# Up projections of two feed-forward stages by seven block products in place of eight, in a decoder layer on one Trainium2 core

## The chip, the cores and the metric

The kernel runs on one core of a Trainium2 chip. The metric is the device time of one execution in microseconds. Three runs of the kernel before took 1301.07 to 1302.55 us, with a median of 1301.34 us.

## The reference

One layer of a decoder: 512 tokens of width 1024, all in float32. Four residual stages follow one another, each closed by a layer norm. The first and the last are SwiGLU feed-forward stages of inner width 2816; between them lie a token mixer (two kinds of attention) and an attention into 256 memory rows. Cut to what matters here:

```python
def swiglu(x, w1, w3, w2):
    return (jax.nn.silu(x @ w1) * (x @ w3)) @ w2

h = layer_norm(ALPHA * h + 0.5 * swiglu(h, ffn1_w1[l], ffn1_w3[l], ffn1_w2[l]), ln1_g[l], ln1_b[l])
mix = parallel_mixer(h, ...)
h = layer_norm(ALPHA * h + mix, ln2_g[l], ln2_b[l])
h = layer_norm(ALPHA * h + memory_attention(h, mem, ...), ln3_g[l], ln3_b[l])
h = layer_norm(ALPHA * h + 0.5 * swiglu(h, ffn2_w1[l], ffn2_w3[l], ffn2_w2[l]), ln4_g[l], ln4_b[l])
```

x is 512 x 1024, w1 and w3 are 1024 x 2816, w2 is 2816 x 1024. "Up projections" are x @ w1 and x @ w3.

## The kernel before

**Numbers in two parts.** TensorE multiplies values of a short float format. So each float32 operand is held as two such parts, a high part and the rest (tiles whose names end in `hl`), and a product takes three matmuls (`mm3`): high by high, high by low, low by high. Each of the three has its own weight load. Making the two parts is a `split`: a CAST to the high part, on ScalarE or VectorE as the planner chooses (`scaled`), and one subtraction on VectorE for the low part.

**The feed-forward stage** (`ffn(n, ...)`, n = 1 for the first stage and n = 4 for the last). The inner width is 22 tiles of 128 columns, numbered f; ten groups hold two tiles each, but the last holds four. For a tile f, `up` computes two products, of `w1[f]` and `w3[f]` with the transposed activations `hT` (8 contraction tiles of 128 channels by 512 tokens): 8 x 3 matmuls of 512 columns each, so 96 for a pair of tiles. `gated` then forms silu (ScalarE), the product with the other half (VectorE, tile `s`) and splits it into `g`. `down` multiplies the g of one group by the matching rows of w2: for 4 token tiles x 2 column halves x 2 tiles of g x 3, 48 matmuls of 512 columns (`res_w` in the trace), and each of the 8 results is added to the residual sums `acc` by VectorE. `up` of group g+1 is issued ahead of `down` of group g, so the tiles g have time to be made.

**Weights.** `Weights` fetches pieces of 128 x 1024 in the order of use: one DMA of 512 KB on SyncE's queue into `w_raw` (3 buffers), then a split into `hl` (pool `wsplit`, 5 buffers of both parts). A new piece is fetched when one is done.

**Order.** The instructions of TensorE come from generators. Those of the other engines wait in a list, and a planner (`Issue` with `Timed`) gives each a duration by its size (`form`) and hands them out in the order in which their data should be there. Each engine then runs its own queue strictly in order, and waits where the data is late.

**Stages in the trace.** Feed-forward stage 1 lies at 10 to 367 us, the mixer and the memory attention behind it, and feed-forward stage 4 at 924 to 1300 us. At the start of stage 4 the first pair of tiles is done by `project_halves`, on 256 tokens and then on the other 256, because the norm of the stage ahead delivers token tiles one after another (`trh` are the transposes of its results). GpSimd only does one small power in each norm (`rs_ln`), its DMA queues are not used.

Nearly all instructions of VectorE, ScalarE and GpSimd stand under one line, L176 (the helper that issues them), all matmuls of `mm3` under L258, transposes under L267.

Of the kernel before, what the change touches and what calls it, by code (L numbers as in the profile page):

```python
# [62 lines left out]
class Issue:  # L63
    """Sets the order of the instructions. Generators issue the tensor engine's; each yields what its next piece waits
    for (nothing, a Mark, or a condition), and of those that could go on the one of the highest rank does. The clock
    counts the rows of the tensor engine. The other engines' instructions are charged by their size and leave when what
    they read should be there, so that none holds up its engine's queue."""
# [94 lines left out]
def form(engine, name, op, args, kw):  # L162
    """Engine, nanoseconds on it and after it, call; then what the call writes and reads."""
# [10 lines left out]
    else:  # L174
        ns = 50.0 if name == "sync" else 120.0 + 80.0 * n
# [3 lines left out]
class Timed:  # L179
    """An engine whose instructions await their turn."""  # L180
# [12 lines left out]
def layer(ctx: ExitStack, tc: tile.TileContext, a: dict, out: bass.AP):  # L193
# [34 lines left out]
    def drop(*tiles):  # L228
        """Nothing issued from here on reads these banks."""
# [10 lines left out]
    def scaled(out, src, scale=None):  # L240
        """out = src * scale on ScalarE or VectorE, whichever ends first."""
# [15 lines left out]
    def matmul(ps, w, x, start, stop):  # L257
        issue.pe(lambda: nc.tensor.matmul(ps, w, x, start=start, stop=stop), ps, w, x)  # L258

    def mm3(ps, w, x, first, last):  # L260
        """(w0 + w1).T @ (x0 + x1) without the product of the two low parts, which lies below float32's last bit."""
        matmul(ps, w[0], x[0], first, False)
        matmul(ps, w[0], x[1], False, False)
        matmul(ps, w[1], x[0], False, last)
# [116 lines left out]
    class Norm:  # L381
# [26 lines left out]
        def turn(self, t, acc):  # L408
            n = self.n
            for half in range(2):  # L410
# [17 lines left out]
    class Residual:  # L428
        """alpha * h plus the products of groups of contraction tiles, then the norm."""
# [39 lines left out]
    # ---------------------------------------------------------------- feed-forward half step  # L469
    groups = [range(2 * g, 2 * g + 2) for g in range(9)] + [range(18, NF)]  # L470

    def plan_ffn(n, w1, w3, w2):
# [4 lines left out]

        up(groups[0])
        for g, fs in enumerate(groups):
            if g + 1 < len(groups):  # L480
                up(groups[g + 1])
# [3 lines left out]
    def ffn(n, src, ready=None):  # L485
        res = Residual(n, src)
        gT = {}
# [741 lines left out]
```

## Time and profile before

| what | value |
|---|---|
| runs | 1301.34 us (1301.07 to 1302.55) |
| span of the profiled execution | 1300.1 us, clock 0.999 |
| what lies around the span, against the median | 1.2 us |
| TensorE busy | 1279.1 us, 98%, 6210 matmuls |
| VectorE busy | 736.5 us, 57% |
| ScalarE busy | 403.7 us, 31% |
| GpSimd busy | 22.8 us, 2% |
| DMA | 142.99 MB, 110 GB/s |

The span runs from the first to the last instruction. Busy time is a mean over the whole execution; the stages differ, so the windows and the chain below it are read by stage.

### The profile page before, as it was taken

How to read it: one execution, taken by the hardware profiler on the slowest of the kernel's cores; microseconds unless marked ns; L12 is line 12 of the kernel's file. 1: busy time of each engine (PE TensorE's matmuls, PEld its weight loads, DVE VectorE, ACT ScalarE, POOL GpSimd, SP SyncE). 2: the span in 40 equal slices, each digit the busy share in tenths (PEclk: the TensorE clock that was granted, in tenths of full speed). 3: DMA queues.
4: the chain of work that ended last, by engine and by line, in shares of the span. 5: the costliest groups of instructions: out<-in, count | busy, mean ns of one | idle time of the engine just before them, and what ended most of it. 6: DMA issues, size and time to landing. Idle time of an engine off the chain costs nothing.

```text
span 1300.1 us, 15614 instructions
## 1 busy us (share of the span) xinstructions
PE 1279.1 (98%) x6210; PEld 1059.8 (82%) x6210; DVE 736.5 (57%) x1250; ACT 403.7 (31%) x670; POOL 22.8 (2%) x33
## 2 busy tenths in 40 slices
PE   7999999999999999999999999999999999999997
PEld 5888887888889987877778898888988888888886
DVE  5444444354482799666657684574754444444446
ACT  3122222121133476334441253451422222222211
POOL 0000000000010000000000000000100000000000
PEclk9999999999999999999999999999999999999999
DMA  7323333243332412232333444234532232332231
GB/s 272 127 97 97 98 97 91 66 146 98 114 110 91 133 50 66 64 115 81 97 98 113 169 171 147 81 125 151 196 124 89 94 97 98 97 97 87 94 96 65
DMA packets 43212, 142.99 MB, mean 110 GB/s; under 512 B 4963, under 2 KB 6755, under 8 KB 43140
## 3 DMA queue, kind: packets, MB, share of 16 engines
q1 hardware_dynamic: 43140, 142.00, 33.6%
q8 instruction: 49, 0.80, 0.3%
q14 instruction: 23, 0.19, 0.0%
HBM read 132.94 MB, written 9.04 MB: 109 GB/s over the span
## 4 chain that ended last, share of the span: by engine, by line
PE 92%; DVE 5%; ACT 1%; DMA 1%; issue 1%; SPq 0%; POOL 0%; DVEq 0%; POOLq 0%; ACTq 0%
PE pw L258 38%; PE res_w L258 18%; PE mq L258 3%; PE res_w_o L258 3%; PE pgd L258 3%; PE res_mem_w_o L258 2%; PE mk L258 2%; PE vd L258 2%; PE qd L258 2%; PE pw_gm L258 2%; PE kd L258 2%; PE mv L258 2%; PE pyd L258 2%; PE cq L258 1%; PE pgm L258 1%; DVE ed L176 1%
## 5 line engine op out<-in xcount | busy, mean ns | idle before, releaser
L258 PE MATMUL pw<-hT,w_hl 128*128 128x512 f32 (+1 forms) x2208 | 502.5, 388 | 6.9 <-DVE w_hl L176 4.7
L258 PEld LDWEIGHTS pw<-hT,w_hl 128*128 128x128 f32 x2208 | 403.8, 189 | 101.8 <-ACT hT L176 7.5
L176 ACT CAST w_hl<-w_raw 128x1024 fp32r<-128x1024 f32 x129 | 133.5, 1050 | 514.5 <-PE pw L258 326.4
L176 DVE TENSOR_TENSOR w_hl<-w_raw,w_hl 128x1024 fp32r<-128x1024 f32 (+1 forms) x134 | 160.0, 1205 | 156.1 <-ACT w_hl L176 155.9
L258 PE MATMUL res_w<-w_hl,g 128*128 128x512 f32 x1056 | 243.3, 390 | 0.0
L258 PEld LDWEIGHTS res_w<-w_hl,g 128*128 128x128 f32 x1056 | 198.0, 188 | 41.8 <-DVE w_hl L176 0.3
L176 DVE TENSOR_TENSOR acc<-acc,res_w 128x512 f32<-128x512 f32 x128 | 85.3, 685 | 50.4 <-PE res_w L258 50.4
L176 DVE SCALAR_TENSOR_TENSOR s<-pw,s 128x512 f32<-128x512 f32 x44 | 30.4, 691 | 141.3 <-PE pw L258 140.6
L258 PE MATMUL pgd<-hT,w_gd_hl 128*128 128x512 f32 x192 | 47.5, 400 | 0.0
L258 PE MATMUL mq<-hT,mem_wq_hl 128*128 128x512 f32 x192 | 46.1, 398 | 0.0
L258 PE MATMUL res_mem_w_o<-mem_w_o_hl,moT 128*128 128x512 f32 x192 | 44.5, 391 | 0.0
L258 PE MATMUL res_w_o<-w_o_hl,zT 128*128 128x512 f32 x192 | 44.5, 391 | 0.0
L258 PEld LDWEIGHTS mq<-hT,mem_wq_hl 128*128 128x128 f32 x192 | 35.8, 188 | 8.3
L258 PEld LDWEIGHTS pgd<-hT,w_gd_hl 128*128 128x128 f32 x192 | 35.5, 188 | 8.4
L258 PEld LDWEIGHTS res_mem_w_o<-mem_w_o_hl,moT 128*128 128x128 f32 x192 | 35.8, 188 | 7.7 <-DVE mem_w_o_hl L176 0.3
L258 PEld LDWEIGHTS res_w_o<-w_o_hl,zT 128*128 128x128 f32 x192 | 35.8, 188 | 7.7 <-DVE w_o_hl L176 0.3
L176 ACT ACTIVATE s<-pw 128x512 f32<-128x512 f32 x44 | 26.0, 591 | 16.6 <-PE pw L258 16.6
L176 POOL TENSOR_TENSOR rs_ln<-ms_ln,mhalf 128x1 f32<-128x1 f32 x16 | 13.4, 836 | 997.7 <-DVE ms_ln L176 997.7
L176 DVE TENSOR_TENSOR g<-s,g 128x512 fp32r<-128x512 f32 x44 | 30.1, 684 | 0.0
L176 DVE SCALAR_TENSOR_TENSOR acc<-acc,res_w 128x512 f32<-128x512 f32 x32 | 21.6, 684 | 13.2 <-PE res_w L258 13.2
L176 ACT ACTIVATE sq<-acc,nmu 128x1024 f32<-128x1024 f32 x16 | 18.5, 1154 | 30.7 <-DVE nmu L176 29.2
L258 PE MATMUL pgm<-hT,w_gm_hl 128*128 128x512 f32 x96 | 24.9, 402 | 0.0
(243 smaller groups left out, 1397.1 us busy)
## 6 DMA issues: line engine op xcount, KB each, us to landing
w_raw<-in_ffn_w SPq DMA_DIRECT2D x131, 512.0 KB, 3.6
h_dram<-acc SPq DMA_DIRECT2D x12, 512.0 KB, 2.7
acc<-h_dram SPq DMA_DIRECT2D x12, 512.0 KB, 5.8
w_gm_raw<-in_w_gate SPq DMA_DIRECT2D x8, 512.0 KB, 3.5
w_gd_raw<-in_w_gate SPq DMA_DIRECT2D x8, 512.0 KB, 3.5
w_o_raw<-in_w_o SPq DMA_DIRECT2D x8, 512.0 KB, 3.5
mem_wk_raw<-in_mem_wk SPq DMA_DIRECT2D x8, 512.0 KB, 4.1
mem_wq_raw<-in_mem_w_q SPq DMA_DIRECT2D x8, 512.0 KB, 4.1
```

What stands on the lines that cost most here:

```text
L176: return (name, ns, 1500.0 if name == "sync" else 0.0, lambda: getattr(engine, op)(*args, **kw)), outs, ins
L258: issue.pe(lambda: nc.tensor.matmul(ps, w, x, start=start, stop=stop), ps, w, x)
```

## The change

Pair 0 of each feed-forward stage (tiles f = 0 and 1) stays as it was. For the pairs 1 to 10 of both stages, 20 in all, the up projections go another way. View the product of a pair as 2 x 2 blocks: two tiles of columns, two halves of the channels (512 each), two halves of the tokens (256 each). `seven` computes it by seven block products in place of eight: each product is 4 contraction tiles x 3 matmuls x 2 weights (w1, w3) = 24 matmuls of 256 columns, 168 for a pair.

- `Pair` loads the four weight blocks b0 to b3 of a pair (each 128 x 1024: 512 channels of one tile of w1, and of w3) by two DMAs of 256 KB each, eight DMAs for a pair instead of four of 512 KB, and the same bytes.
- `make` forms the operand of a product ahead of its split: b0 += b1 for product 5 and b0 += b3 for product 6 on VectorE, b1 += b3 for product 7 and b0 += b2 for product 4 on GpSimd, all 128 x 1024 in place. The blocks go through 7 splits for a pair in place of 4.
- `sums_of_h` forms, once for each stage, four sums of blocks of the activations (S for products 5, 6 and 3, and S3 for product 7) from float32 copies `h_raw`: in stage 1 the loaded `xT` tiles, in stage 4 four slots that ScalarE fills by 16 more copies of 128 x 256 out of the transposes of norm 3. That is 8 operations of 128 x 512 on VectorE, and 8 splits.
- `seven` copies products 1 and 5 and the sum of 1 and 6 out of PSUM (ScalarE, 128 x 512), adds them to later products by three VectorE operations, and makes silu and gate in four halves of 256 tokens.
- The planner charges large GpSimd operations 100 + 2.2 ns for each column. This is a number in the planner's table, not a measurement shown here.

The core of the diff (lines that only lose a comment are left out):

```diff
-        ns = 50.0 if name == "sync" else 120.0 + 80.0 * n
+        ns = 50.0 if name == "sync" else 120.0 + 80.0 * n if n < 8 else 100.0 + 2.2 * n
...
+        def load(self, *blocks):
+            for i in blocks:
+                if i not in self.b:
+                    self.b[i] = slot(f"{self.name}_b{i}", F32, [P, 1024])
+                    for w, src in enumerate(self.src):
+                        sp.dma_start(self.b[i][:, w * 512:w * 512 + 512], src[i % 2][:, i // 2 * 512:i // 2 * 512 + 512])
...
+        def make(self, i, hl):
+            b = self.b
+            if i == 1:
+                self.load(0, 1, 3, 2)
+            if self.after and i in (3, 2):
+                self.after.load(*((0, 1) if i == 3 else (3, 2)))
+            for at, other in {5: ((0, 1),), 6: ((0, 3),), 7: ((1, 3),), 4: ((0, 2),)}.get(i, ()):
+                (pool if i in (7, 4) else dve).tensor_tensor(b[at], b[at], b[other], op=ALU.add)
+            src = b[{1: 0, 5: 0, 6: 0, 4: 0, 3: 3, 7: 1, 2: 2}[i]]
+            split(hl[:, 0], hl[:, 1], src)
...
+    ORDER = (1, 5, 6, 3, 7, 2, 4)
...
+                dve.tensor_tensor(a, low[:, :, two], up[:, :, two], op=ALU.subtract)
+                split(views[0][:, kk, 0], views[0][:, kk, 1], a)
+                dve.scalar_tensor_tensor(b, a, -1.0, up[:, :, one], op0=ALU.mult, op1=ALU.subtract)
+                split(views[1][:, kk, 0], views[1][:, kk, 1], b)
+                dve.scalar_tensor_tensor(c, b, -1.0, low[:, :, one], op0=ALU.mult, op1=ALU.subtract)
+                split(views[j][:, 4:6, 0], views[j][:, 4:6, 1], c)
+                dve.tensor_tensor(a, up[:, :, one], up[:, :, two], op=ALU.subtract)
+                split(s3[j][:, :, 0], s3[j][:, :, 1], a)
...
+        def seven(p):
...
+            def product(ps, i, first):
+                hl = W.take(f"wp{n}_{p}_{i}")
+                for w in range(2):
+                    for k in range(4):
+                        o = w * 512 + k * P
+                        mm3(ps[:, w * 256:(w + 1) * 256], hl_of(hl, slice(o, o + P)), sums[i](k),
+                            first and w == 0 and k == 0, w == 1 and k == 3, not first)
+                W.done(f"wp{n}_{p}_{i}")
...
+            x = bank(f"px{n}_{p}")
+            product(x, 1, True)
+            p1 = wk(f"p1_{n}_{p}")
+            act.copy(p1, x)
...
+            product(z, 3, False)
+            dve.tensor_tensor(u2, u2, z, op=ALU.add)
+            drop(z)
+            out(gw[1][:, one], u2, -1.0)
+            yield
+            product(x, 7, False)
+            dve.tensor_tensor(p5, p5, x, op=ALU.add)
+            out(gw[1][:, two], p5, -1.0)
+            gT[f1] = slot(f"g{n}_{f1}")
+            split(gT[f1][:, 0], gT[f1][:, 1], gw[1])
...
         for g in range(len(groups)):
             if g + 1 < len(groups):
-                yield from up(groups[g + 1])
+                for f in groups[g + 1][::2]:
+                    yield from seven(f // 2)
             yield from down(g)
```

**What moves, first place.** TensorE's queue at the fourth pair of stage 1 (f = 8 and 9), in the kernel before; pw1 and pw3 are the products of w1 and w3, each row is a run of equal matmuls:

```order
L258 MATMUL pw1_1_8_910<-hT0_89,w1_1_8_hl_762 128x512 x12
L258 MATMUL pw1_1_8_910<-hT1_90,w1_1_8_hl_762 128x512 x12
L258 MATMUL pw3_1_8_942<-hT0_89,w3_1_8_hl_798 128x512 x12
L258 MATMUL pw3_1_8_942<-hT1_90,w3_1_8_hl_798 128x512 x12
L258 MATMUL pw1_1_9_974<-hT0_89,w1_1_9_hl_828 128x512 x12
L258 MATMUL pw1_1_9_974<-hT1_90,w1_1_9_hl_828 128x512 x12
L258 MATMUL pw3_1_9_1008<-hT0_89,w3_1_9_hl_901 128x512 x12
L258 MATMUL pw3_1_9_1008<-hT1_90,w3_1_9_hl_901 128x512 x12
```

and in the changed kernel (px, pz and py are the three PSUM banks of a pair, `wp1_4_1_hl` is the split operand of product 1 of pair 4 in stage 1):

```order
L258 MATMUL px1_4_1259<-hT0_89,wp1_4_1_hl_1105 128x256 x24
L258 MATMUL pz1_4_1296<-S1_0_114,wp1_4_5_hl_1137 128x256 x24
L258 MATMUL px1_4_1259<-S1_1_115,wp1_4_6_hl_1169 128x256 x24
L258 MATMUL pz1_4_1296<-S1_0_114,wp1_4_3_hl_1244 128x256 x6
L258 MATMUL pz1_4_1296<-S1_1_115,wp1_4_3_hl_1244 128x256 x6
...
L258 MATMUL px1_4_1259<-S3_1_0_116,wp1_4_7_hl_1247 128x256 x6
L258 MATMUL px1_4_1259<-S3_1_1_117,wp1_4_7_hl_1247 128x256 x6
...
L258 MATMUL py1_4_1419<-hT1_90,wp1_4_2_hl_1284 128x256 x24
L258 MATMUL px1_4_1259<-hT1_90,wp1_4_4_hl_1321 128x256 x24
```

In place of 96 matmuls of 512 columns stand 168 of 256, and px is read back by ScalarE or VectorE between its products.

**Second place.** VectorE's queue over the same stretch, before: the subtractions of four weight pieces and two w2 pieces and the gates of one pair of tiles, up to the next group's sums, some of it for the pair that follows:

```order
L176 TENSOR_TENSOR w3_1_7_hl_695<-w3_1_7_raw_694,w3_1_7_hl_695 128x1024
L176 TENSOR_TENSOR w2_1_4_hl_697<-w2_1_4_raw_696,w2_1_4_hl_697 128x1024
L176 TENSOR_TENSOR w2_1_5_hl_732<-w2_1_5_raw_731,w2_1_5_hl_732 128x1024
L176 SCALAR_TENSOR_TENSOR s1_6_766<-pw3_1_6_736,s1_6_766 128x512
L176 CAST g1_6_767<-s1_6_766 128x512
L176 TENSOR_TENSOR w1_1_8_hl_762<-w1_1_8_raw_761,w1_1_8_hl_762 128x1024
L176 TENSOR_TENSOR g1_6_767<-s1_6_766,g1_6_767 128x512
L176 TENSOR_TENSOR w3_1_8_hl_798<-w3_1_8_raw_797,w3_1_8_hl_798 128x1024
L176 SCALAR_TENSOR_TENSOR s1_7_832<-pw3_1_7_802,s1_7_832 128x512
L176 CAST g1_7_833<-s1_7_832 128x512
L176 TENSOR_TENSOR w1_1_9_hl_828<-w1_1_9_raw_827,w1_1_9_hl_828 128x1024
L176 TENSOR_TENSOR g1_7_833<-s1_7_832,g1_7_833 128x512
```

and in the changed kernel, from behind the residual adds of group 1 (pair 3's products 3, 7, 2 and 4) to the first add of the next group, with pair 4's operands between:

```order
L176 TENSOR_TENSOR wp1_3_3_hl_937<-wp1_3_b3_671,wp1_3_3_hl_937 128x1024
L176 TENSOR_TENSOR wp1_3_7_hl_940<-wp1_3_b1_632,wp1_3_7_hl_940 128x1024
L176 TENSOR_TENSOR wp1_3_2_hl_977<-wp1_3_b2_672,wp1_3_2_hl_977 128x1024
L176 TENSOR_TENSOR wp1_3_4_hl_1014<-wp1_3_b0_631,wp1_3_4_hl_1014 128x1024
...
L176 TENSOR_TENSOR p5_1_3_1015<-p5_1_3_1015,px1_3_952 128x512
L176 TENSOR_TENSOR wp1_4_1_hl_1105<-wp1_4_b0_938,wp1_4_1_hl_1105 128x1024
L176 SCALAR_TENSOR_TENSOR gw1_3_1_951<-p5_1_3_1015,gw1_3_1_951 128x256
L176 TENSOR_TENSOR wp1_4_b0_938<-wp1_4_b0_938,wp1_4_b1_939 128x1024
L176 CAST wp1_4_5_hl_1137<-wp1_4_b0_938 128x1024
...
L176 TENSOR_TENSOR wp1_4_5_hl_1137<-wp1_4_b0_938,wp1_4_5_hl_1137 128x1024
L176 TENSOR_TENSOR wp1_4_b0_938<-wp1_4_b0_938,wp1_4_b3_978 128x1024
...
L176 TENSOR_TENSOR wp1_4_6_hl_1169<-wp1_4_b0_938,wp1_4_6_hl_1169 128x1024
L176 TENSOR_TENSOR acc1_0_330<-acc1_0_330,res1_w2_1_4_0_0_1177 128x512
```

The subtractions of seven pieces and the two sums now share the queue with the adds that empty px, pz and py. `wp1_3_b1` and `wp1_3_b0`, read by the second and the fourth row, were written by GpSimd's two sums. TensorE's product 4 writes px again and so waits for the row that adds px to `p5`.

**Third place.** VectorE's queue at the start of stage 4, behind the last transposes of norm 3 (`trh3_3`), before:

```order
L176 TENSOR_TENSOR hT0_89<-trh3_3_0_7685,hT0_89 128x4x128
L176 TENSOR_TENSOR hT1_90<-trh3_3_1_7690,hT1_90 128x4x128
L176 TENSOR_TENSOR w3_4_2_hl_7737<-w3_4_2_raw_7736,w3_4_2_hl_7737 128x1024
L176 SCALAR_TENSOR_TENSOR s4_0_7825<-pw3_4_0_7585,s4_0_7825 128x512
L176 CAST g4_0_7826<-s4_0_7825 128x512
L176 TENSOR_TENSOR w1_4_3_hl_7766<-w1_4_3_raw_7765,w1_4_3_hl_7766 128x1024
L176 TENSOR_TENSOR g4_0_7826<-s4_0_7825,g4_0_7826 128x512
L176 TENSOR_TENSOR w3_4_3_hl_7795<-w3_4_3_raw_7794,w3_4_3_hl_7795 128x1024
```

and in the changed kernel:

```order
L176 TENSOR_TENSOR hT1_90<-trh3_3_1_8734,hT1_90 128x4x128
L176 TENSOR_TENSOR hT0_89<-trh3_3_0_8729,hT0_89 128x4x128
L176 CAST wp4_1_5_hl_8809<-wp4_1_b0_8608 128x1024
L176 TENSOR_TENSOR S4_0a_8907<-hraw2_8407,hraw0_8405 128x512
L176 TENSOR_TENSOR wp4_1_5_hl_8809<-wp4_1_b0_8608,wp4_1_5_hl_8809 128x1024
L176 TENSOR_TENSOR S4_1a_8910<-hraw3_8408,hraw1_8406 128x512
L176 TENSOR_TENSOR wp4_1_b0_8608<-wp4_1_b0_8608,wp4_1_b3_8610 128x1024
L176 SCALAR_TENSOR_TENSOR s4_0_8899<-pw3_4_0_8650,s4_0_8899 128x512
L176 CAST wp4_1_6_hl_8837<-wp4_1_b0_8608 128x1024
L176 TENSOR_TENSOR wp4_1_6_hl_8837<-wp4_1_b0_8608,wp4_1_6_hl_8837 128x1024
...
L176 TENSOR_TENSOR S4_0_8903<-S4_1a_8910,S4_0_8903 128x2x256
L176 TENSOR_TENSOR wp4_1_2_hl_8979<-wp4_1_b2_8611,wp4_1_2_hl_8979 128x1024
```

The sums of the activations, their splits and the operands of pair 1 stand there now, among the gates of pair 0. The last row but one is the last part that product 5 reads, in its third and fourth contraction tile; the last row is the operand of product 2.

## Rows read from the trace of the kernel before

**Rows 1.** The page: busy time of each engine; the chain that ended last, by engine, then by line.

```profile
span 1300.1 us, 15614 instructions
...
PE 1279.1 (98%) x6210; PEld 1059.8 (82%) x6210; DVE 736.5 (57%) x1250; ACT 403.7 (31%) x670; POOL 22.8 (2%) x33
...
PE 92%; DVE 5%; ACT 1%; DMA 1%; issue 1%; SPq 0%; POOL 0%; DVEq 0%; POOLq 0%; ACTq 0%
PE pw L258 38%; PE res_w L258 18%; PE mq L258 3%; PE res_w_o L258 3%; PE pgd L258 3%; PE res_mem_w_o L258 2%; PE mk L258 2%; PE vd L258 2%; PE qd L258 2%; PE pw_gm L258 2%; PE kd L258 2%; PE mv L258 2%; PE pyd L258 2%; PE cq L258 1%; PE pgm L258 1%; DVE ed L176 1%
```

**Rows 2.** The chain that ended last: start, duration (us), engine, tile, line, count.

```profile
66.96 22.49 PE pw L258 x96
89.45 10.89 PE res_w L258 x48
...
302.14 44.97 PE pw L258 x192
...
382.48 9.86 PE pw_gm L258 x84
...
769.95 14.39 PE mk L258 x120
...
934.82 35.31 PE pw L258 x204
```

**Rows 3.** Windows: one pair and its down products, in stage 1 and stage 4.

```profile
core 0: us, PE busy (x) PEld busy (x) DVE busy (x) ACT busy (x) POOL busy (x), PEclk, DMA share, GB/s
66.96:100.34 33.38, 33.38 (x146) 27.09 (x145) 15.69 (x20) 7.19 (x9) 0.00 (x0) 1.00 0.29 95
1014.41:1047.79 33.38, 33.38 (x145) 27.09 (x145) 15.69 (x20) 7.19 (x9) 0.00 (x0) 1.00 0.28 95
```

**Rows 4.** Groups by shape, weight loads: busy us, mean ns | idle before.

```profile
L258 PEld LDWEIGHTS pw<-hT,w_hl 128*128 128x128 f32 x2208 | 403.8, 189 | 101.8 <-ACT hT L176 7.5 <-DVE hT L176 1.7 <-issue 0.5
...
L258 PEld LDWEIGHTS mk<-memT,mem_wk_hl 128*128 128x128 f32 x192 | 23.1, 192 | 0.0
L258 PEld LDWEIGHTS pw_gm<-hT,w_gm_hl 128*128 128x128 f32 x192 | 22.7, 188 | 0.0
```

**Rows 5.** Groups by shape, VectorE.

```profile
L176 DVE TENSOR_TENSOR w_hl<-w_raw,w_hl 128x1024 fp32r<-128x1024 f32 x131 | 158.5, 1220 | 156.0 <-ACT w_hl L176 155.9
L176 DVE TENSOR_TENSOR acc<-acc,res_w 128x512 f32<-128x512 f32 x128 | 85.3, 685 | 50.4 <-PE res_w L258 50.4
...
L176 DVE CAST g<-s 128x512 fp32r<-128x512 f32 x44 | 18.8, 426 | 1.4
...
L176 DVE TENSOR_TENSOR ptx<-trx,ptx 128x256 fp32r<-128x256 f32 x16 | 5.9, 416 | 0.1
...
L176 DVE CAST w_hl<-w_raw 128x1024 fp32r<-128x1024 f32 x2 | 1.4, 690 | 4.2 <-PE pw L258 4.2
```

**Rows 6.** GpSimd's timeline: start, duration (us), operation, idle before.

```profile
583.07 1.02 POOL L176 TENSOR_TENSOR rs_od<-ms_od,mhalf 128x4 f32<-128x4 f32 x1 [143.44 <-DVE ms_od L176]
...
919.86 0.55 POOL L176 TENSOR_TENSOR rs_ln<-ms_ln,mhalf 128x1 f32<-128x1 f32 x1 [5.80 <-DVE ms_ln L176]
928.65 2.53 POOL L176 TENSOR_TENSOR rs_ln<-ms_ln,mhalf 128x1 f32<-128x1 f32 x1 [8.24 <-DVE ms_ln L176]
```

**Rows 7.** VectorE's timeline at the start of stage 4, same columns.

```profile
928.43 2.35 DVE L176 TENSOR_TENSOR w_hl<-w_raw,w_hl 128x1024 fp32r<-128x1024 f32 x2
931.22 1.28 DVE L176 SCALAR_TENSOR_TENSOR acc<-u,rs_ln,lnb 128x1024 f32<-128x1024 f32 x1 [0.44 <-POOL rs_ln L176]
935.03 1.29 DVE L176 TENSOR_TENSOR hT<-trh,hT 128x512 fp32r<-128x512 f32 x2 [2.53 <-ACT hT L176]
940.21 1.22 DVE L176 TENSOR_TENSOR w_hl<-w_raw,w_hl 128x1024 fp32r<-128x1024 f32 x1 [3.89 <-ACT w_hl L176]
```

**Rows 8.** DMA issues: count, KB each, median us to landing.

```profile
w_raw<-in_ffn_w SPq DMA_DIRECT2D x131, 512.0 KB, 3.6
...
out<-acc SPq DMA_DIRECT2D x8, 256.0 KB, 2.0
```

More of the change, by code (lines that the diff above doesn't have):

```diff
@@ L255, in split, with matmul, mm3 @@
             dve.scalar_tensor_tensor(lo, src, scale, f32(hi), op0=ALU.mult, op1=ALU.subtract)
[L257 to L264, printed above, removed]
+    def matmul(ps, w, x, start, stop, again=False):
+        issue.pe(lambda: nc.tensor.matmul(ps, w, x, start=start, stop=stop, skip_group_check=again), ps, w, x)
+    def mm3(ps, w, x, first, last, again=False):
+        matmul(ps, w[0], x[0], first, False, again)
+        matmul(ps, w[0], x[1], False, False, again)
+        matmul(ps, w[1], x[0], False, last, again)
     def transpose(ps, src):
@@ L283, in fetch @@
             key, src = self.specs.pop(0)
+            if callable(src):
+                hl = wsplit.tile([P, 2, 1024], F32R, tag="hl", name=f"{key}_hl")
+                with issue.delayed(LATER):
+                    src(hl)
+                self.tiles[key] = hl
+                self.held += 1
+                return
             n = src.shape[1]
@@ L415, in turn @@
                 split(dst[:, :, 0], dst[:, :, 1], ps.rearrange("p (k t) -> p k t", k=4))
+                if n == 3:
+                    for j in range(2):
+                        act.copy(h_raw[2 * half + j][:, :, t * P:(t + 1) * P], ps[:, j * 256:(j + 1) * 256].rearrange("p (k t) -> p k t", k=2))
                 drop(ps)
@@ new lines, in layer, with sums_of_h @@
+    ORDER = (1, 5, 6, 3, 7, 2, 4)
+    def sums_of_h(n, sums):
+        pts = [ppool.tile([P, 2, 13, P], F32R, tag="pt", name=f"S{n}_{i}").rearrange("p a b c -> p (a b c)") for i in range(2)]
+        views = [t[:, :3072].rearrange("p (k i t) -> p k i t", k=6, i=2) for t in pts]
+        s3 = [slot(f"S3_{n}_{i}") .rearrange("p k (i t) -> p k i t", i=2) for i in range(2)]
+        sums[5] = lambda k: [views[0][:, k, i] for i in (0, 1)]
+        sums[6] = lambda k: [views[1][:, k, i] for i in (0, 1)]
+        sums[3] = lambda k: [views[k // 2][:, 4 + k % 2, i] for i in (0, 1)]
+        sums[7] = lambda k: [s3[k // 2][:, k % 2, i] for i in (0, 1)]
+        one, two = slice(0, 256), slice(256, 512)
+        with issue.delayed(LATER):
+            for j in range(2):
+                up, low = h_raw[j], h_raw[2 + j]
+                kk = slice(2 * j, 2 * j + 2)
+                a, b, c = [wk(f"S{n}_{j}{i}").rearrange("p (k t) -> p k t", k=2) for i in "abc"]
+                dve.tensor_tensor(a, low[:, :, two], up[:, :, two], op=ALU.subtract)
[6 more added lines that the diff above has]
+                split(s3[j][:, :, 0], s3[j][:, :, 1], a)
+        mark = issue.when(views[0], views[1], s3[0], s3[1])
+        h_raw.clear()
+        for i, (k0, toks) in {1: (0, one), 2: (4, one), 4: (4, two)}.items():
+            sums[i] = lambda k, k0=k0, toks=toks: hk(k0 + k, toks)
+        return mark
@@ L479, in plan_ffn @@
+    def plan_ffn(n, w1, w3, w2):
+        for f in groups[0]:
+            W.plan(f"w1_{n}_{f}", w1[f])
+            W.plan(f"w3_{n}_{f}", w3[f])
+        pairs = [Pair(f"wp{n}_{p}", [w[2 * p:2 * p + 2] for w in (w1, w3)]) for p in range(1, NF // 2)]
+        for p, q in zip(pairs, pairs[1:]):
+            p.after = q
         for g, fs in enumerate(groups):
             if g + 1 < len(groups):
-                up(groups[g + 1])
+                for f in groups[g + 1][::2]:
+                    pairs[f // 2 - 1].plan()
@@ L505, in up, with out @@
                 gated(f, *ps)
+        def seven(p):
+            x, y, z = None, None, None
+            def product(ps, i, first):
[6 more added lines that the diff above has]
+                W.done(f"wp{n}_{p}_{i}")
+            def out(dst, c, sign):
+                act.activation(dst, c[:, :256], AF.Silu, scale=sign)
+                dve.scalar_tensor_tensor(dst, c[:, 256:], 0.5 * sign, dst, op0=ALU.mult, op1=ALU.mult)
+            one, two = slice(0, 256), slice(256, 512)
+            gw = [wk(f"gw{n}_{p}_{i}") for i in range(2)]
+            f0, f1 = 2 * p, 2 * p + 1
+            x = bank(f"px{n}_{p}")
[3 more added lines that the diff above has]
+            yield
+            z = bank(f"pz{n}_{p}")
+            product(z, 5, True)
+            p5 = wk(f"p5_{n}_{p}")
+            act.copy(p5, z)
+            yield
+            product(x, 6, False)
+            u2 = wk(f"u2_{n}_{p}")
+            act.copy(u2, x)
+            yield
+            product(z, 3, False)
+            dve.tensor_tensor(u2, u2, z, op=ALU.add)
+            drop(z)
+            out(gw[1][:, one], u2, -1.0)
+            yield
+            product(x, 7, False)
[3 more added lines that the diff above has]
+            split(gT[f1][:, 0], gT[f1][:, 1], gw[1])
+            yield
+            y = bank(f"py{n}_{p}")
+            product(y, 2, True)
+            dve.tensor_tensor(p1, p1, y, op=ALU.add)
+            drop(y)
+            out(gw[0][:, one], p1, 1.0)
+            yield
+            product(x, 4, False)
+            out(gw[0][:, two], x, 1.0)
+            drop(x)
+            gT[f0] = slot(f"g{n}_{f0}")
+            split(gT[f0][:, 0], gT[f0][:, 1], gw[0])
+            yield
         def down(g):
@@ L983, in out_proj @@
         for m in sizes:
+            if n == 3 and k0 + m == KT:
+                h_raw.extend(slot(f"hraw{j}", F32) for j in range(4))
             if n == 2 and k0 + m == KT:
```

26 lines of the change are left out of this document (18 added, 8 removed).

## The prediction

> **What bounds the kernel now.** I read the page first, for the engine that the end hangs on: TensorE is busy for 98% of a span of 1300.1 us, and 92% of the chain that ended last are its matmuls, 38% up projections (`pw`) and 18% down products (`res_w`) [rows 1]. The chain in order of time then says how the two feed-forward stages run: 96 matmuls of a pair of tiles in 22.49 us, 48 down products in 10.89 us, and so on without a gap [rows 2]. The windows of one such pair say what stands beside: in 33.38 us TensorE is busy all the time at a granted clock of 1.00, VectorE for 15.69 us, ScalarE for 7.19 us, GpSimd not at all, DMA at 0.28 to 0.29 [rows 3]. So time leaves only if TensorE's work does, and everything that is added must fit beside it.
>
> **What is removed.** Before, 96 matmuls of 512 columns take 22.49 us, 234.3 ns each. After, 168 of 256 columns; their price decides the gain. The trace has such matmuls: `pw_gm` with hT moving, 84 in 9.86 us or 117.4 ns, and `mk` with memT moving, 120 in 14.39 us or 119.9 ns [rows 2]. 117.4 is almost exactly half of 234.3. The weight loads have no idle time left at 256 columns, where those of `pw` have 101.8 us [rows 4], but the rate did not suffer for it. All at 117.4 a pair would take 19.72 us, all at 119.9 it would take 20.14. I take 117.4 for products 1, 2 and 4 (72 matmuls that move hT) and 119.9 for the 96 that move sums, since these are small separate tiles as memT is: 8.45 + 11.51 = 19.96 us. That saves 2.53 us for a pair (bounds 2.35 and 2.77). Ten pairs in each of two stages: **50.6 us** (47.0 to 55.4). The down products stay, so the new period is 19.96 + 10.89 = 30.85 us.
>
> **What VectorE gets, per pair.** Seven weight and two w2 subtractions at 1.22 us, 10.98; two sums of the same size at the same price, 2.44; four casts of 1024 columns that the planner moved here, at 0.69, 2.76; three adds out of PSUM and two subtractions of g at the price of the residual adds, 0.685, 3.43; four half-width gates at 0.416, 1.66; one cast of g, 0.43; eight residual adds, 5.48 [rows 5]. Sum 27.2 us of 30.85, after 15.69 of 33.38. Two subtractions back to back took 2.35 us, not 2.44 [rows 7], so the true need lies a little lower. It fits, but VectorE runs in order, and its waits matter. Laid out from the first matmul of product 1: the operand of 3 is ready at 2.4 to 5.3 us and read at about 8.5; the add of px to `p5` is done at 15.4 to 15.9, and product 4, which writes px again, starts at about 17. This margin of 1 to 1.5 us is the smallest; the banks for the next pair and the last down product have 2 to 3. I cost VectorE at nothing in the steady state, and hidden by TensorE; if the cover is gone, each microsecond of lag costs 20 over the kernel.
>
> **ScalarE** has about five casts, three copies and four half-width silus: 12 at 0.80 us, the mean of the window's nine in 7.19 [rows 3], some 10 us of 30.85. It costs nothing, except where a cast waits for GpSimd.
>
> **GpSimd** gets two sums of 128 x 1024 per pair, 40 in all, and no such row exists. From below: the same sum on VectorE, 1.22 us [rows 5]. From above: its power takes 0.55 us for one column and 1.02 for four [rows 6], 0.157 us for each further column, which would be 160 us for 1024. I take twice VectorE, 2.4 us: an add is nearer to VectorE's add than to a power, whose cost per column is that of a function. The sum for product 4 can start when VectorE has split the operand of 6 (at about 27 us of the period at the latest) and must end at 6.7 us of the next, for behind the cast of 4 on ScalarE stands the copy of product 5, for which TensorE waits at product 3. The window is about 10 us; that of the sum for 7 is larger. So at 2.4 us it costs nothing.
>
> How the two engines share their access shows in one row. While VectorE ran two subtractions with both inputs in SBUF (2.35 us), GpSimd's power of 0.55 took 2.53 [rows 6, 7]: GpSimd was held until they ended. Nothing in the trace shows VectorE held by GpSimd; its instructions beside that power kept their length. The Trainium skill, "SBUF — State Buffer", section "Who interferes with whom", says that the two share a port pair as an exclusive lock, the holder for its whole instruction; the held power agrees. It also says that it works in both directions, which no row here shows. What that would do is the first rival. The Trainium skill, "GPSIMD Engine Reference", section "Elementwise — side-by-side cycle accounting", measures an add of 2048 float32 columns at 4497 ns against 2293 on VectorE; half of it would be an estimate of 2.25 us, with the same sum.
>
> **DMA.** Eight transfers of 256 KB in place of four of 512: a 256 KB write lands in 2.0 us, a 512 KB load in 3.6 [rows 8], so the bytes take about as long, at a share of 0.28. They are requested half a pair ahead; SyncE issues four more in 30 us. Nothing.
>
> **One-off costs.**
> - Start of stage 1: two subtractions for the sums stand ahead of the last splits of hT on VectorE (2 x 0.685 us), and product 5 may wait for the last sum's split: 2.5 us (1 to 5).
> - Pair 8 of stage 1: the tables that are issued there push the operands of products 1, 5 and 6 behind the sixth residual add. Between it and the seventh stand six operations (two casts, three subtractions, a sum; 4.9 us by [rows 5]), and product 5's subtraction follows the eighth. By that count product 5 waits 3 us (1 to 5).
> - Start of stage 4: VectorE's hT subtractions end at 936.3 us and it then had 3.89 us of idle before 940.21 [rows 7]. The change puts 25 operations there up to the last part that product 5 reads. By size they are 18 to 19.6 us, and about 2 us go in waiting for pair 0's gate: 954 to 957.5. TensorE reaches that point at 951: of the 204 matmuls from 934.82 on [rows 2], 108 are pair 0's, of 256 columns, 12.7 us; product 1 takes 2.8 and the first seven matmuls of product 5 0.8. A wait of 3 to 6.5, and up to 3 for the blocks' transfers, as one cast of them now stands ahead of norm 3's last tile: 6 us (2 to 13).
>
> **Sum.** 1300.1 - 50.6 + 2.5 + 3 + 6 = 1261.0 us of span. The median of the runs is 1.2 us above the profiled span: **1262 us**, 3.0% less.
>
> **The rivals.**
> - *VectorE becomes the bound.* If GpSimd's two sums hold VectorE for 2.4 us each, its need is 27.2 + 4.8 = 32 us against 30.85, up to 1.2 us for a pair; if, besides that, a wait in its queue makes `p5` late by its margin, 1.5 more. For it speaks the held power, against it that the sum for 4 runs while VectorE does residual adds, which read PSUM, and that its waits early in the period absorb lag. I take 0.7 us a pair (0.4 to 1.2): 1262 + 14 = 1276 (1270 to 1285). Chance 0.22.
> - *The starts cost nothing and all matmuls run at 117.4 ns*: 1300.1 - 55.4 + 1.2 = 1246, and with half of the one-off costs 1252. The separate tiles of memT speak against it. Chance 0.09.
> - *GpSimd is too slow.* This is the one that makes it slower than before. It decides at about 10 us for a sum, from which TensorE waits in each pair; the gain is gone at about 12 (39 us over 20 pairs, 2 each). At 20 us for a sum it would be 1262 + 20 x 10 = 1462. For it speaks only the slope of the power, against it VectorE's add. Chance 0.06.
> - *The gain is eaten*: waits of 2 us in each pair, 1300. It needs the hold's 1.2 us and half of the margin on top, in each pair. Chance 0.02.
>
> The forecast itself keeps 0.61, from 1254 to 1269.
>
> **Range and chances.** From 1249, between the second rival and the lower end of the forecast, to 1285, the end of the first: outside lie some of the second rival, the third, the fourth and what I have not seen, under 2 in 10. A change of 0.2%, 2.6 us, is about what a measurement of this kernel can tell from none. Faster by more: 0.61 + 0.22 + 0.09 = 0.92. Within 0.2%: 0.02. Slower: 0.06.
>
> **What would show it.** In the chain, steady pairs of 168 matmuls in 19.7 to 20.2 us and 48 in 10.89, with no other engine between; a window of a pair of 30.9 us with VectorE at 25 to 28. GpSimd's 40 sums at 2 to 3 us each; at more than 10 the third rival. VectorE's subtractions longer than 1.22 us beside GpSimd's sums would show that GpSimd holds VectorE. At stage 4 a wait of TensorE for `S` of some 6 us once. The prediction is wrong if 256-column matmuls on S tiles cost more than 120 ns, or if VectorE stands in the chain of each pair.

## The result and the profile after

The changed kernel takes **1269.49 us** (median of 4 runs, 1268.33 to 1270.81) against 1301.56 us for the kernel before (median of 4 runs, the three of the table above and one more): a ratio of 0.9754 (95% interval 0.974 to 0.9768). The profiled execution took 1269.63 us, with a span of 1267.8 us. The forecast was 1262 us (1249 to 1285): the direction and the range held, the size is 7.5 us off.

From the page of the changed kernel, which answers to [rows 1]:

```profile
PE 1236.8 (98%) x7650; PEld 1103.5 (87%) x7650; DVE 1008.1 (80%) x1539; ACT 452.0 (36%) x805; POOL 131.9 (10%) x73
...
PE 87%; DVE 9%; ACT 1%; issue 1%; DMA 1%; SPq 0%; POOL 0%; DVEq 0%; POOLq 0%; ACTq 0%
...
L176 DVE TENSOR_TENSOR wp_hl<-wp_b,wp_hl 128x1024 fp32r<-128x1024 f32 x140 | 187.1, 1362 | 9.8 <-ACT wp_hl L176 9.7
L176 POOL TENSOR_TENSOR wp_b<-wp_b,wp_b 128x1024 f32<-128x1024 f32 x40 | 110.2, 2756 | 501.8 <-DVE wp_b L176 217.0
```

A pair in the chain that ended last, in stage 4; it answers to [rows 2]:

```profile
1001.30 2.85 PE px L258 x24
1004.15 2.87 PE pz L258 x24
1007.03 2.88 PE px L258 x24
1009.91 2.88 PE pz L258 x24
1012.79 2.88 PE px L258 x24
1015.67 2.82 PE py L258 x24
1018.49 2.82 PE px L258 x24
1021.30 10.93 PE res_w L258 x48
```

The 168 matmuls take 20.00 us (forecast 19.96), and nothing stands between them. Products on S run at 2.88 / 24 = 120.0 ns a matmul, those on hT at 117.5. The windows of that pair, of pair 8 of stage 1 and of the start of stage 4 (two stretches) answer to [rows 3]:

```profile
core 0: us, PE busy (x) PEld busy (x) DVE busy (x) ACT busy (x) POOL busy (x), PEclk, DMA share, GB/s
1001.30:1032.23 30.93, 30.93 (x219) 29.01 (x218) 28.66 (x36) 8.76 (x14) 5.39 (x2) 1.00 0.31 103
259.50:266.20 6.70, 5.56 (x25) 5.27 (x26) 6.60 (x7) 1.39 (x2) 1.79 (x1) 0.51 0.00 0
936.40:944.20 7.80, 4.32 (x18) 3.89 (x19) 7.80 (x12) 2.22 (x4) 1.56 (x1) 0.66 0.00 0
944.20:951.80 7.60, 7.60 (x58) 7.39 (x57) 4.86 (x6) 2.65 (x4) 0.00 (x0) 0.90 0.00 0
```

In the steady pair TensorE has no idle time and VectorE needs 28.66 of 30.93 us. In pair 8 and in the first stretch of stage 4 VectorE is busy nearly all the time (6.60 of 6.70 us, 7.80 of 7.80), TensorE is not, and its granted clock is 0.51 and 0.66; in the second stretch of stage 4 it is 0.90.

VectorE's and GpSimd's timelines in that pair answer to [rows 6, 7]; first VectorE, three of its rows:

```profile
1021.06 2.84 DVE L176 TENSOR_TENSOR wp_hl<-wp_b,wp_hl 128x1024 fp32r<-128x1024 f32 x1
1023.82 0.68 DVE L176 TENSOR_TENSOR g<-gw,g 128x512 fp32r<-128x512 f32 x1
...
1028.56 2.51 DVE L176 TENSOR_TENSOR g<-gw,g 128x512 fp32r<-128x512 f32 x1
```

and GpSimd:

```profile
1019.82 2.99 POOL L176 TENSOR_TENSOR wp_b<-wp_b,wp_b 128x1024 f32<-128x1024 f32 x1 [19.64 <-DMA wp_b<-in_ffn_w]
1028.11 2.40 POOL L176 TENSOR_TENSOR wp_b<-wp_b,wp_b 128x1024 f32<-128x1024 f32 x1 [5.30 <-DVE wp_hl L176]
```

Beside each of GpSimd's two sums one VectorE instruction that reads only SBUF is held: a subtraction of 1.22 us takes 2.84, one of 0.68 takes 2.51, and each ends about its own length behind the end of GpSimd's sum (1022.81 and 1030.51). That is 1.6 + 1.8 = 3.4 us of VectorE for this pair. Two inputs are not needed: in other pairs it is a CAST of one tile that is held, 0.69 us becoming 2.6 to 2.9.

The hold stands in TensorE's waits at three places. At the start of stage 1 a subtraction for the sums takes 2.47 us instead of 0.69, and TensorE waits 2.01 us for it; at pair 8 a CAST takes 2.62 us, and TensorE waits 2.03 us for its piece:

```profile
36.06 2.37 POOL L176 TENSOR_TENSOR wp_b<-wp_b,wp_b 128x1024 f32<-128x1024 f32 x1 [6.98 <-DVE wp_hl L176]
36.51 2.47 DVE L176 TENSOR_TENSOR S<-S_1a,S 128x512 fp32r<-128x512 f32 x1
39.04 2.29 PE L258 MATMUL pz<-S,wp_hl 128*128 128x256 f32 x17 [2.01 <-DVE S L176]
...
256.44 2.36 POOL L176 TENSOR_TENSOR wp_b<-wp_b,wp_b 128x1024 f32<-128x1024 f32 x1 [36.62 <-DVE wp_b L176]
256.73 2.62 DVE L176 CAST wp_hl<-wp_b 128x1024 fp32r<-128x1024 f32 x1
259.41 0.59 PE L258 MATMUL pz<-S,wp_hl 128*128 128x256 f32 x2 [2.03 <-DVE wp_hl L176]
```

At the start of stage 4 both engines are held. While VectorE runs one operation with two SBUF inputs after another, a sum of GpSimd takes 6.78 us; beside its end an operation of VectorE takes 2.27 us instead of 0.69. A CAST of ScalarE waits for that operation; its copy of product 1 out of px stands behind the CAST and then waits 0.59 us for one more subtraction of VectorE. For this copy TensorE waits 3.45 us:

```profile
931.18 6.78 POOL L176 TENSOR_TENSOR wp_b<-wp_b,wp_b 128x1024 f32<-128x1024 f32 x1 [9.49 <-DVE wp_hl L176]
936.24 2.27 DVE L176 SCALAR_TENSOR_TENSOR S_0c<-S_0b,hraw 128x512 f32<-128x512 f32 x1
938.54 0.62 ACT L176 CAST S<-S_0c 128x512 fp32r<-128x512 f32 x1 [1.12 <-DVE S_0c L176]
939.75 0.59 ACT L176 COPY p<-px 128x512 f32<-128x512 f32 x1 [0.59 <-DVE S L176]
940.38 3.86 PE L258 MATMUL px<-S,wp_hl 128*128 128x256 f32 x15 [3.45 <-ACT p L176]
```

**Where the time went**, by the starts of the down products in the two traces. The pairs give 2.455 us each (33.38 to 30.925, the two first ones 2.49), 49.2 us in all. Four places take 17.0 us back: the start of stage 1 2.35 us (the first down products begin at 55.92 instead of 56.07), pair 8 of stage 1 6.7 (its seven products take 26.9 us instead of 20.0, and 0.15 of that was there before), the start of stage 4 7.1 (50.7 us from its first matmul to its first down product, 46.1 before, and the 2.49 that the pair should have given), and pair 10, which follows pair 9 with no down products between, 0.4 in stage 1 and 0.5 in stage 4. 49.2 - 17.0 = 32.2; the spans differ by 32.3.

### The profile page after: what moved, and what is told of

It reads as the page before. It is cut to its first block, busy times and chain, and to the rows that moved or that the text cites. A ratio compares the mean times of both kernels' runs of the same rounds, so it can differ in the third digit from the quotient of the medians.

```text
span 1267.8 us, 19130 instructions
## 1 busy us (share of the span) xinstructions
PE 1236.8 (98%) x7650; PEld 1103.5 (87%) x7650; DVE 1008.1 (80%) x1539; ACT 452.0 (36%) x805; POOL 131.9 (10%) x73
## 4 chain that ended last, share of the span: by engine, by line
PE 87%; DVE 9%; ACT 1%; issue 1%; DMA 1%; SPq 0%; POOL 0%; DVEq 0%; POOLq 0%; ACTq 0%
PE res_w L258 19%; PE px L258 17%; PE pz L258 9%; PE py L258 4%; PE mq L258 4%; PE res_w_o L258 3%; PE res_mem_w_o L258 3%; PE pgd L258 3%; DVE wp_hl L176 2%; PE mk L258 2%; PE vd L258 2%; PE pw_gm L258 2%; PE qd L258 2%; PE kd L258 2%; PE mv L258 2%; PE pyd L258 2%
## 5 line engine op out<-in xcount | busy, mean ns | idle before, releaser
L176 DVE TENSOR_TENSOR wp_hl<-wp_b,wp_hl 128x1024 fp32r<-128x1024 f32 x140 | 187.1, 1362 | 9.8 <-ACT wp_hl L176 9.7
L176 POOL TENSOR_TENSOR wp_b<-wp_b,wp_b 128x1024 f32<-128x1024 f32 x40 | 110.2, 2756 | 501.8 <-DVE wp_b L176 217.0
L258 PE MATMUL pz<-S,wp_hl 128*128 128x256 f32 x960 | 125.4, 287 | 5.2 <-DVE wp_hl L176 3.2
L258 PE MATMUL px<-S,wp_hl 128*128 128x256 f32 x960 | 124.1, 286 | 3.5 <-ACT p L176 3.5
L176 ACT CAST wp_hl<-wp_b 128x1024 fp32r<-128x1024 f32 x84 | 86.6, 1051 | 112.3 <-PE res_w L258 53.1
L258 PEld LDWEIGHTS pz<-S,wp_hl 128*128 128x128 f32 x960 | 121.0, 196 | 6.1 <-DVE wp_hl L176 3.7
L258 PEld LDWEIGHTS px<-S,wp_hl 128*128 128x128 f32 x960 | 119.9, 194 | 4.1 <-ACT p L176 3.9
L258 PE MATMUL px<-hT,wp_hl 128*128 128x256 f32 x960 | 119.9, 281 | 1.0 <-DVE p L176 0.5
L258 PEld LDWEIGHTS px<-hT,wp_hl 128*128 128x128 f32 x960 | 117.1, 188 | 3.0 <-DVE p L176 0.9
L258 PEld LDWEIGHTS pw<-hT,w_hl 128*128 128x128 f32 x288 | 42.4, 195 | 13.4 <-ACT hT L176 7.3
```

The costliest lines, as they stand in the source:

```text
L176: return (name, ns, 1500.0 if name == "sync" else 0.0, lambda: getattr(engine, op)(*args, **kw)), outs, ins
```

## The experiments

**Theory.** GpSimd and VectorE hold each other. In steady pairs the hold is hidden, at the places where VectorE is what TensorE waits for it is paid, and behind the waits of pair 8 and of stage 4 TensorE's clock is lower as well. **Rivals.** The hold costs something in every pair; or VectorE's load alone, or late block loads, make the places slow.

**1. All four sums on VectorE.**

```diff
-                (pool if i in (7, 4) else dve).tensor_tensor(b[at], b[at], b[other], op=ALU.add)
+                dve.tensor_tensor(b[at], b[at], b[other], op=ALU.add)
```

> All four sums of a pair on VectorE, none on GpSimd. Theory (GpSimd's sum holds VectorE as long as VectorE's own sum would take): in a steady pair of the changed kernel two VectorE instructions are longer by 1.6 and 1.8 us beside GpSimd's sums, 3.4 us; two more sums cost 2.3 to 2.4. So VectorE falls from 28.7 to about 27.5 us in the window of a pair, pairs stay at 30.92 us, and the time stays within 2 us of the changed kernel, 1268 to 1271 us. Rival (GpSimd relieves VectorE): VectorE rises to 31, it comes into the chain of each pair, and the time is 1275 us or more.

1261.43 us (1260.38 to 1262.78), ratio to the kernel before 0.9692 (0.9677 to 0.9706). The window of a steady pair:

```profile
1012.04:1042.97 30.93, 30.93 (x218) 29.01 (x217) 27.26 (x36) 8.76 (x14) 0.00 (x0) 1.00 0.30 99
```

VectorE fell as foreseen, to 27.26 us, although it does two more sums, and the pair stayed. So the rival falls, and VectorE's load alone is not what makes the places slow, for its work grew. That the time would stay was wrong: the span fell by 9.3 us. It fell where VectorE is late: 2.0 us at the start of stage 1, 4.7 from there to the end of stage 1's pairs (pair 8 above all), 2.6 at the start of stage 4 and 0.6 at its pair 10, less 0.6 elsewhere. At the start of stage 1 the subtraction for the sums takes 0.69 us again and TensorE's wait of 2.01 us is gone. So GpSimd's sums have a price, but not in steady pairs. The sums that move also change the order that the planner gives VectorE's queue; what that is worth by itself was not tried.

**2. All four sums on GpSimd.** The same line with `pool.tensor_tensor` for all.

> All four sums of a pair on GpSimd. Theory of the hold: four sums of 2.4 to 3.0 us, and VectorE held by about 1.7 us for each while it runs operations with two inputs in SBUF, so that VectorE stays at 28.5 to 30 us in the window of a pair although two sums of 1.22 us left it; product 5 and 6 then wait for GpSimd in some pairs: 1272 to 1300 us. Rival (GpSimd relieves VectorE): VectorE at 26.2 us in a pair and the time at most that of the changed kernel, 1265 to 1269 us.

1281.2 us (1281.06 to 1282.2), ratio 0.9846 (0.9829 to 0.9862). The window of a steady pair:

```profile
1031.76:1062.68 30.92, 30.92 (x217) 29.00 (x217) 27.27 (x31) 10.12 (x15) 9.83 (x5) 1.00 0.32 102
```

VectorE gave away two sums (2.4 us) and fell by 1.4 only, less than relief would give (26.2) and more than I had expected. Three of the four sums hold it: two CASTs of 0.42 us take 2.17 and 2.50 us, a subtraction of 0.69 takes 2.30. The fourth runs beside residual adds, which read PSUM, and holds nothing. Steady pairs again take 30.92 us. The 11.5 us against the changed kernel were lost at the start of stage 1 (4.7), in its pairs 6 to 10 (5.4) and in small pieces, where the chain now goes through GpSimd's sums.

**3. The tables later.** The bias table and lambda are formed behind the last pair of stage 1.

```diff
         consts()
+        later = Mark()
+        later.floor = 325000.0
+        yield later
         bias_table()
```

> The bias table and lambda are issued some 125 us later, behind the last pair of stage 1; the rest is the changed kernel. Theory (the write of the bias table waits on SyncE's queue and holds back the block loads of pair 8 behind it, so VectorE's operands for it stand behind six residual adds; TensorE waits 3.7 us and its clock is lower for 6 us after): pair 8 falls from 26.9 to 20.0 us, 1262.5 us (1261.5 to 1264). Rival (VectorE's backlog is what makes pair 8 late): a wait of the same size stays, 1267 us or more.

1264.76 us (1264.16 to 1266.85). Pair 8 falls to 20.0 us, as the theory said: all steady distances of stage 1 are 30.92 to 30.93 us. But in the profiled execution 3.6 us are lost again between the end of stage 1's pairs and the memory attention, where the tables now lie among the pieces of norm 1, and 1.6 at the start of stage 4. The place was right, the cure was not.

**4. Pair 1 of stage 4 by eight products.**

```diff
+                    if n == 4 and f == 2:
+                        for e in (2, 3):
+                            W.plan(f"w1_{n}_{e}", w1[e])
+                            W.plan(f"w3_{n}_{e}", w3[e])
+                    else:
+                        pairs[f // 2 - 1].plan()
...
+                if ready and g == 0:
+                    yield from up(groups[1])
+                    yield mark
```

> Pair 1 of stage 4 by eight products as in the kernel before, the other 19 pairs by seven. Theory (the wait of 3.8 us and the lower clock after it at the start of stage 4 come from 25 VectorE operations that must lie ahead of product 5 of the first changed pair): the start falls by 7 us, the pair costs 2.45 us more: 1265 us (1263.5 to 1266.5). Rival (the sums and the operands are late whichever pair comes first): the wait moves to pair 2, 1269 to 1273 us.

1264.54 us (1263.8 to 1264.77), against 1265 expected. The chain at the start of stage 4 has no wait left:

```profile
908.16 7.04 PE pw L258 x60
915.20 0.87 PE trh L267 x8
916.08 38.16 PE pw L258 x228
954.24 10.92 PE res_w L258 x48
965.16 2.85 PE px L258 x24
```

46.1 us up to the down products, as before the change, and pair 2 starts at once. So the sums need about a pair's time ahead of the first changed pair; here an unchanged pair gives it to them.

**5. Sums on VectorE in six pairs only**, those at the places: the condition of experiment 1 gets `and self.name not in ("wp1_1", "wp4_1", "wp1_8", "wp1_9", "wp1_10", "wp4_10")`.

> GpSimd's two sums go to VectorE in six of the twenty pairs only: pair 1 of both stages, pairs 8, 9 and 10 of stage 1 and pair 10 of stage 4; the other fourteen pairs keep them on GpSimd. Theory (the hold costs time only where VectorE is what TensorE waits for, at the two starts and around pair 8, and nothing in steady pairs): as with all sums on VectorE, 1261.4 us, span 1258.5 (1257.5 to 1260). Rival (each of the twenty pairs pays a part): 1266 to 1267 us.

1258.34 us (1256.6 to 1259.04), ratio 0.9667 (0.9653 to 0.9681): the whole gain of experiment 1, and 3 us more, where I had expected the same. The fourteen other pairs pay nothing for the hold:

```profile
1008.70:1039.63 30.93, 30.93 (x218) 29.01 (x217) 28.16 (x33) 8.76 (x13) 5.46 (x3) 1.00 0.30 100
```

The rival that every pair pays falls. The further gain lies in stage 1 (268.9 us between the first down products of its first and of its last group instead of 271.5), where pair 7 keeps its two sums off VectorE just ahead of pair 8; that this is its cause was not tried by itself.

**6. Only the write of the bias table later**, GpSimd's sums as in the change. In the changed kernel SyncE's queue holds two of pair 8's eight block loads ahead of that write; the other six, and pair 9's, wait behind it for VectorE:

```profile
205.85 0.85 SPq L176 DMA_DIRECT2D wp_b<-in_ffn_w  x2
222.77 0.81 SPq L176 DMA_DIRECT2D bias_dram<-rows  x1
223.63 19.97 SPq L176 DMA_DIRECT2D wp_b<-in_ffn_w  x14
```

```diff
+        later = Mark()
+        later.floor = 232000.0
+        yield later
         sp.dma_start(bias_dram.rearrange("h (p m) -> h p m", p=32), rows.unsqueeze(1).broadcast_to([8, 32, REL]))
...
         consts()
-        bias_table()
         lam_calc()
+        yield from bias_table()
```

> The changed kernel with GpSimd's sums as they are; only the write of the bias table is issued behind the block loads of pair 8. Theory (the loads behind that write set pair 8 late; the hold only makes it worse there): pair 8 falls from 26.9 to 20.0 us, nothing is lost elsewhere: 1262.6 us (1261.5 to 1264). Rival (the hold alone would still stop TensorE at pair 8): 1265 us or more.

1263.16 us (1262.99 to 1264.48). All eight loads now stand ahead of the write, which itself goes out at the same time as before, and pair 8 runs from 253.95 to 273.95:

```profile
205.88 11.30 SPq L176 DMA_DIRECT2D wp_b<-in_ffn_w  x8
222.78 0.80 SPq L176 DMA_DIRECT2D bias_dram<-rows  x1
223.69 14.55 SPq L176 DMA_DIRECT2D wp_b<-in_ffn_w  x8
```

So pair 8's 6.7 us come from one wait in SyncE's queue. Without the hold the same lateness costs some 4 us less (experiment 1): the queue is the cause, the hold its multiplier.

**7. Sums on VectorE, the later write and pair 1 by eight, together** (edits of 1, 4 and 6).

> All sums on VectorE; the write of the bias table is issued behind the block loads of pair 8; pair 1 of stage 4 by eight products. Theory: against all sums on VectorE alone (1261.4 us) pair 8 loses its last 2.75 us of delay and the start of stage 4 another 1.9: 1256.8 us (1255.5 to 1258.5). Rival (what remains at pair 8 is VectorE's load, not the loads of its blocks): 1259 us or more.

1255.82 us (1255.65 to 1257.38), ratio 0.9652 (0.9638 to 0.9667), and a span of 1253.7. Nineteen pairs at 2.455 would give 46.6 us of the 1300.1; the span is 46.4 shorter. So what the places take back together is down from 17.0 us to some tenths of a us.

**8 and 9. Does a boundary of 64 bytes make the two rates?** On top of experiment 1, first the sums of the activations 40 bytes further in their tiles, then two constants ahead of hT padded:

```diff
-        views = [t[:, :3072].rearrange("p (k i t) -> p k i t", k=6, i=2) for t in pts]
+        views = [t[:, 10:3082].rearrange("p (k i t) -> p k i t", k=6, i=2) for t in pts]
```

```diff
-    small = const.tile([P, 22], F32, name="small")
+    small = const.tile([P, 32], F32, name="small")[:, :22]
-    mhalf = const.tile([P, 4], F32, name="mhalf")
+    mhalf = const.tile([P, 16], F32, name="mhalf")[:, :4]
```

> All sums on VectorE, and the sums of the activations for products 5, 6 and 3 begin 40 bytes further in their tiles, so that they lie to a boundary of 64 bytes as hT does by its place behind the small constants. Theory (whether the moving tile begins on a boundary makes the 119.9 against 117.4 ns): 72 matmuls per pair fall from 120.0 to 117.4 ns, a pair from 30.93 to 30.74 us, 3.7 us in all: 1257.7 us. Rival (the place makes no difference): 120.0 ns, 1261.4 us.

> All sums on VectorE, and two small constants are padded so that hT begins on a boundary of 64 bytes. Theory (the boundary makes the rate): matmuls that move 512 columns of hT fall from 234.2 to about 226.9 ns, as those that move weights have it, and those of 256 columns rise from 117.4 to 119.9; 768 of the first and some 1800 of the second kind: 1 us less, 1260 us. Rival (the place makes no difference): both rates stay.

1262.58 us (1260.85 to 1264.03) and 1263.05 us (1262.35 to 1263.41). Products on the shifted S still take 2.86 to 2.87 us (119.2 to 119.6 ns), those on the padded hT still 117.4 (84 of `pw_gm` in 9.86 us). The theory of the boundary of 64 bytes falls; no other boundary was tried.

**10 and 11. hT elsewhere.** Only the pool of hT changes, first in the kernel before, then in the version of experiment 7:

```diff
+    high = ctx.enter_context(tc.tile_pool(name="high", bufs=1))
...
-    hT = [const.tile([P, 4, 2, S], F32R, name=f"hT{i}") for i in range(2)]
+    hT = [high.tile([P, 4, 2, S], F32R, name=f"hT{i}") for i in range(2)]
```

> The kernel before, with hT in a pool of its own behind all others instead of among the small constants; the instructions and their order are the same. Theory (the place of hT in SBUF makes its matmuls run at another rate than those that move weights or other tiles): matmuls of 512 columns of hT fall from 234.3 to 226.9 ns; some 2700 of them, 20 us less, 1281 us; those of 256 columns rise from 117.4 to 119.9. Rival (the place makes no difference): 1301 us, both rates as before.

> The version with all sums on VectorE, the later write of the bias table and pair 1 of stage 4 by eight products (1255.8 us), with hT in a pool of its own behind all others. Theory (the place sets the rate): 864 matmuls of 512 columns of hT lose 7.4 ns each, 6.4 us, and some 1750 of 256 columns gain 2.5 ns each, 4.4 us: 1253.8 us (1252.5 to 1255.5). Rival (256 columns of hT stay at 117.4 ns wherever it lies): 1249.4 us.

The kernel before falls to 1283.39 us (1283.28 to 1284.02), ratio 0.986 (0.9845 to 0.9875), with the same instructions. Its chain:

```profile
65.85 21.76 PE pw L259 x96
87.61 10.88 PE res_w L259 x48
...
374.79 10.07 PE pw_gm L259 x84
...
530.24 10.96 PE vd L259 x48
...
759.95 14.39 PE mk L259 x120
```

512 columns of hT now take 226.7 ns, 256 columns 119.9. The pools behind the constants move down by the size of hT too, but matmuls without hT keep their rate: `mk` 14.39 us as in [rows 2], `res_w` 10.88 after 10.89. hT counts where it is the stationary operand as well: `vd` moves its weights against a stationary hT, and its 48 matmuls took 11.26 us before (234.6 ns each, now 228.3):

```profile
538.07 11.26 PE vd L258 x48
```

The version of experiment 7 falls to 1253.95 us (1253.51 to 1254.4), ratio 0.9635 (0.9619 to 0.9651), the fastest that was run; each of its products takes 2.87 or 2.88 us. Why the place matters stays open.

## Why the prediction was right in its direction and 7.5 us off

- **Matmuls, 50.6 us:** 49.2 measured. The rates were right, from `mk` and `pw_gm`; the first product of a pair is 0.03 us slower and the down products behind a pair take 10.93 instead of 10.89.
- **VectorE hidden in the steady state:** right. It needs 28.66 us of 30.93. The 27.2 that were summed had no hold in them, and without it the need is about 25: 27.26 in experiment 1, less two sums that lay on GpSimd in the forecast. So the sum was some 2 us too high, which makes up for more than half of the hold; that it came near is luck.
- **GpSimd at 2.4 us a sum:** near: 2.4 to 3.4 us for 39 of the 40, 6.78 for the one at the start of stage 4. That it "costs nothing" is **the step that failed**. I weighed the hold only against the period of a pair, as the first rival. Its condition came true, with 3.4 us a pair instead of 4.8, but there it is hidden. It costs 9.3 us (experiment 1) at the starts and at pairs 8 to 10, where I had sized VectorE's work without it. Without it the places cost some 7.6 us (1258.5 us of span against 1300.1 - 49.2), where 11.5 were summed: what I had put too high there made up for part of the step, and so the forecast missed by less than the step's 9.3. No row of before showed this direction of the hold. The Trainium skill, "SBUF — State Buffer", section "Who interferes with whom", says that either of the two engines can be the one that waits, by which of them issues first; the trace after agrees, with 0.68 us becoming 2.51 on VectorE and 2.4 becoming 6.78 on GpSimd.
- **Start of stage 1, 2.5 us:** 2.35. 2.0 of it is the hold, not the order that I had argued from, so the size is right by luck.
- **Pair 8, 3 us:** 6.7. I read the late operands in VectorE's order and did not look for what made the planner set them there and the loads late: the write in SyncE's queue (experiment 6).
- **Start of stage 4, 6 us:** 7.1. TensorE waited 0.3 + 3.45 us, inside the 3 to 6.5 of the forecast, but not for `S`: it waited for ScalarE's copy of product 1. Matmuls of products 2 and 6 stand in its queue ahead of the rest of product 5, and while they ran VectorE ended the part of `S` that this rest reads (943.06). What the waits do not explain is mostly the lower clock behind them, for which I had no term: 15 matmuls in 3.86 us there, 1.80 at the usual rate.
- **Pairs 9 and 10 back to back:** not costed, 0.9 us for both stages; its cause was not looked for.
- **DMA and ScalarE:** hidden, as said. A 256 KB block lands in 6.0 us instead of 2.0, without harm in steady pairs.

By these terms the span is some 7 us over the forecast of 1261.0, and 6.8 by measurement; most of what is left of the 7.5 lies around the span (1.7 us instead of 1.2).

The waits of TensorE in the changed kernel (us in total, times, longest) hold most of what is not the clock: the first is at the start of stage 4, the second at pair 8, the third at the start of stage 1.

```profile
PE px L258 <- ACT p L176: 3.5, 1, 3.5
...
PE pz L258 <- DVE wp_hl L176: 3.2, 2, 2.0
PE pz L258 <- DVE S L176: 2.0, 1, 2.0
```

## What to carry to other kernels

Work that fits beside the bound in the steady state is still paid at the starts and wherever a queue makes an operand late; cost it there, with the slower durations that it has beside another engine. An engine that relieves another while holding it relieves nothing: measure the held instruction, not the moved one. Before a product is rewritten, compare the rate of its matmuls with others of the same shape: 18 us lay in the place of one tile.

## What the runs showed of the hardware that I had not expected

- GpSimd's sum of two SBUF tiles holds a VectorE instruction that works from SBUF to SBUF: a subtraction takes 2.84 us instead of 1.22 or 2.51 instead of 0.68, and a CAST of one tile 2.62 instead of 0.69. VectorE's adds out of PSUM beside it keep their 0.68. The other way round, a sum of GpSimd took 6.78 us beside VectorE's operations.
- In the 6.7 us that begin behind a wait of 2.0 us and hold another of 1.1 us TensorE's granted clock was 0.51, that is about the lower level of 1.2 GHz; at the start of stage 4 it was 0.66, then 0.90. Behind the wait of 2.01 us at the start of stage 1 it stayed at 1.00.
- Matmuls that move hT take 234.3 ns for 512 columns and 117.4 for 256 where hT lies among the constants, 226.7 and 119.9 where it lies behind the other pools. By that, a pair by eight products takes 32.64 us and one by seven 31.06: the change is worth 1.58 us a pair there, not 2.46. In all it is 29.4 us (1283.39 against 1253.95), with the three cures of experiment 7.
